# Query-chunk and value-row stores moved between the GpSimd and SP queues, and the second attention head loaded later, in a hybrid attention layer

## The chip, the cores and the metric

The kernel runs on one core of a Trainium2 chip. The metric is the device time of one execution in microseconds; a kernel's time is the median of its runs. The engines are named as the profile names them: PE is TensorE (matrix products into PSUM banks), PEld its weight loads, DVE is VectorE, ACT is ScalarE, POOL is GpSimd, SP is SyncE, which only issues transfers. A transfer is issued by an instruction on one of these engines. Those that SP issues are in the profile's DMA queue q1, those that GpSimd issues in q0; sixteen DMA engines carry both.

## The reference

One layer of a decoder trunk on 1024 tokens of width 1024 with 16 meta tokens ahead of them, all in float32. One input projection feeds two groups of heads: four gated-DeltaNet heads and eight forgetting-attention heads of width 64. One output projection takes both, then comes a SwiGLU network of inner width 2816 and a last norm:

```
u = rmsnorm(h, attn_norm_w[l])
proj = u @ w_in[l]
gq, gk, gv, gz, gb, ga, fq, fk, fv, ff = jnp.split(proj, IN_SPLITS, axis=-1)
o_gdn = gated_deltanet_group(...)
o_fox = forgetting_attention_group(fq, fk, fv, ff, fgate_b[l])
h = h + jnp.concatenate([o_gdn, o_fox], axis=-1) @ w_out[l]
h = h + swiglu(rmsnorm(h, ffn_norm_w[l]), w_gate[l], w_up[l], w_down[l])
h = rmsnorm(h, final_norm_w)
return h[:, N_META:]
```

and in the attention group, by blocks of 128 queries (the meta tokens are a block of their own),

```
sc = einsum("bqhd,bkhd->bhqk", q[:, s:e], k[:, :e]) * scale + c[:, :, s:e, None] - c[:, :, None, :e]
p = softmax(where(causal, sc, MASK_VALUE), axis=-1)
outs.append(einsum("bhqk,bkhd->bqhd", p, v[:, :e]))
```

where `c` is the running sum of the logarithms of the forget gates.

## The kernel before

Each float32 product is made of three products of rounded parts: a value is split into a high part (`hi`, a cast on ACT) and a low part (`lo`, a subtraction on DVE), and PE adds hi·hi, hi·lo and lo·hi into one PSUM bank.

The program runs in stages: the DeltaNet projections (0 to 230 us of the span); the attention heads' value projection in two blocks of four heads, `fv1` (230 to 259.5) and `fv0` (259.5 to 285); their key projection `fk` (to 345), with the DeltaNet group's triangular solves (`py`, `pu`) between its matmuls; their query projection `fq` (to 433.5), with the DeltaNet group's eight scan chunks between; the attention (to some 580), in which output-projection matmuls of the DeltaNet half (`wog`) fill the gaps; the rest of the output projection (to 658); and the SwiGLU network.

The order of PE's instructions is set by a small planner (`PeOrder`, L45): chains of work with due times are taken when due, and a filler (`fox()`, the attention heads' projections, later `wog`) is taken otherwise. PE takes that order as it stands. On the other engines and the queues the order is the scheduler's, which takes instructions by priority as their inputs come. `tc.issue_after(x)` puts what is issued in its scope behind the instruction `x` on the engine on which `x` is queued; it is an order on that queue and does not wait for the transfer to land.

What the change touches:

- `fox_proj` (L762) projects keys, then queries. For each pair of heads `m` (0 to 3) and each of three column chunks it fills a PSUM bank (`pj_fq`), splits it into the tile `fhl_fq{m}_{c0}` (ACT L777, DVE L778; two buffers) and stores that to a DRAM scratch, `k_d` or `q_d` (L780, on GpSimd). The three PSUM banks that `ps_mm` hands out in turn are shared with `wog`. The names in the rows are `fhl_fq2_358` for pair 2, column 358, and so on; `fq3_700` is the last.
- The value blocks (L937 to L959) come as nine row tiles each: the 16 meta rows (tile -1) and eight of 128 tokens. Each is split into a tile `fvt` (three buffers) and stored to DRAM: the meta rows by four small stores to `vz_d` (L953), the others to `v_d` (L957), on SP. `vst[0]` holds the last such store; the loads of the key projection's weights (`raw_fk0`, `raw_fk1`), and `ubk` and `na` of the solves (L605 to L608), are issued behind it.
- `att_tiles(i)` (L725) makes the score operands `ka{i}` and `qa{i}` and fills six rows of each with constants on GpSimd (L727, L728). `att_head(h)` (L739) loads a head on SP: the gate sums into `ka` and `qa`, two halves each of `kk` and `sa`, the rest of `ka` and `qa`, the values `avt`, and then the meta values `vm0`/`vm1` (`vm_load`, L736; head 1 brings those of heads 0 and 1). The buffers alternate between even and odd heads. The scores read `ka`, `qa`, `kk`, `sa`; the products with the meta rows' probabilities (`phm`) read `vm`, the others `avt`.
- `wout_gdn` (L1179) loads a tile of the input `x` as `ht` (L1190, GpSimd), runs twelve `wog` matmuls, adds the one to the other on DVE (L1193) and stores the sum to `h_d` (L1194, GpSimd).
- `zmask` (L1013, L1014) is the causal mask of the scores, filled on GpSimd; the casts `whi_wo` and `wlo_wo` (L168, L169) split output-projection weights into the buffers in which the query projection's weights were.

Of the kernel before, what the change touches and what calls it, by code (L numbers as in the profile page):

```python
# [9 lines left out]
F32 = mybir.dt.float32  # L10
# [11 lines left out]
NT = S // P  # L22
# [75 lines left out]
def tile_hymba_layer(ctx, tc, x, meta, attn_norm_w, w_in, conv_w, a_log, dt_bias, gdn_norm_w,  # L98
                     fgate_b, w_out, ffn_norm_w, w_gate, w_up, w_down, final_norm_w, out):
    nc = tc.nc  # L100
    x, out, w_in, conv_w = x[0], out[0], w_in[0], conv_w[0]
# [12 lines left out]
    def ps_mm(name):  # L114
        rot[0] = rot[0] % 3 + 1 if rot[0] else 0
        return ps_v(name) if rot[0] > 1 else bank("mm", 1, name)
# [34 lines left out]
    v_d = dram.tile([FH, T, P], F32, name="v_d")  # L151
# [58 lines left out]
    def mm3g(dst, pairs, us):  # L210
        n = len(pairs)
        for i, (lh, ll, rh, rl) in enumerate(pairs):
            for a, b, first, last in ((lh, rh, i == 0, False), (lh, rl, False, False), (ll, rh, False, i == n - 1)):
                nc.tensor.matmul(dst, a, b, start=first, stop=last)  # L214
                od.pe(us)
                yield
# [56 lines left out]
    def tok_cols(t):  # L273
        return (0, NM) if t < 0 else (NM + P * t, P)
# [431 lines left out]
    def proj_tmg(acc, t, w, n):  # L706
        col, rows = tok_cols(t)
        yield from mm3g(acc[:rows, :n], [(uh[:, k, col:col + rows], ul[:, k, col:col + rows], w[0][k][:, :n],
                                          w[1][k][:, :n]) for k in range(KT)], n / 2400)

    last, vst = [None], [None]
# [5 lines left out]
    def fox_load():  # L717
        if fox_ws:
            with tc.issue_after(vst[0].ins) if vst[0] and not last[0] else nullcontext():
                fox_w.append(win_block(*fox_ws.pop(0)))  # L720

    t_ld, hds, fixed, fq_m, h_ld = [], {}, [], [0], {}

    def att_tiles(i):
        ka = als[i].tile([NA + DH, T], F32R, name=f"ka{i}")  # L725
        qa = als[i].tile([NA + DH, S], F32R, name=f"qa{i}")
        nc.gpsimd.memset(ka[:NA].bitcast(F32), 1.0)  # L727
        nc.gpsimd.memset(qa[:NA].bitcast(F32), -1.0)  # L728
        fixed.append((ka, qa))
# [4 lines left out]
    def vm_load(h):  # L734
        for i in range(2):
            h_ld[h] = nc.sync.dma_start(vms[h % 2][NR * i:NR * i + NR].rearrange("p j c -> p (j c)").bitcast(F32),  # L736
                                        vz_d[h, 0:NR * 512].rearrange("(p f) -> p f", f=512))

    def att_head(h):  # L739
        m, hb = h // 2, h % 2  # L740
        rows = slice(DH * hb, DH * hb + DH)
        al_ = als[h % 2]
        kk = al_.tile([P, T], F32R, tag="kk", name=f"kk_{h}")
        sa = al_.tile([P, S], F32R, tag="sa", name=f"sa_{h}")
        ka, qa = fixed[h % 2]
        nc.sync.dma_start(ka[3:NA].bitcast(F32), c_d[h])
        nc.sync.dma_start(qa[0:3].bitcast(F32), c_d[h, :, NM:T])
        for i in range(2):
            half = slice(DH * i, DH * i + DH)
            nc.sync.dma_start(kk[half].bitcast(F32), k_d[m, rows, 0])  # L750
            nc.sync.dma_start(sa[half].bitcast(F32), q_d[m, i, rows])
        nc.sync.dma_start(ka[NA:].bitcast(F32), k_d[m, rows, 1])
        nc.sync.dma_start(qa[NA:].bitcast(F32), q_d[m, 0, rows])
        vt = al_.tile([P, NT, P], F32R, tag="vt", name=f"avt_{h}")
        nc.sync.dma_start(vt.bitcast(F32), v_d[h, NM:T].rearrange("(t p) d -> p t d", p=P))
        t_ld.append(od.t)
        if h:
            for i in (0, 1) if h == 1 else (h,):
                vm_load(i)
        return m, rows, kk, sa, ka, qa, vt  # L760

    def fox_proj(dst, chunks, off, scale, nm):  # L762
        for b in range(2):
            w = fox_w.pop(0)
            for i in range(2):
                m = 2 * b + i
                for ci, (c0, n) in enumerate(chunks):
                    if (i, ci) == (0, 1):
                        fox_load()
                    acc = ps_mm(f"pj_{nm}{m}_{c0}")  # L770
                    yield from mm3g(acc[:, :n], [(w[0][k][:, P * i:P * i + P], w[1][k][:, P * i:P * i + P],
                                                  uh[:, k, c0:c0 + n], ul[:, k, c0:c0 + n])
                                                 for k in range(KT)], n / 2400)
                    od.on("act", n / 1200)
                    od.on("dve", n / 900)
                    hl = fp.tile([P, 2, 348], F32R, tag="fhl", name=f"fhl_{nm}{m}_{c0}")
                    nc.scalar.activation(hl[:, 0, :n], acc[:, :n], AF.Copy, scale=scale)  # L777
                    nc.vector.scalar_tensor_tensor(hl[:, 1, :n], acc[:, :n], scale, hl[:, 0, :n].bitcast(F32),  # L778
                                                   op0=ALU.mult, op1=ALU.subtract)
                    last[0] = nc.gpsimd.dma_start(dst(m)[:, :, c0 - off:c0 - off + n], hl[:, :, :n].bitcast(F32))  # L780
                    if off:
                        fq_m[0] = m

# [28 lines left out]
    ra_ld = {}  # L812
# [116 lines left out]
    def fox():  # L929
        fox_load()  # L930
        w = fox_w.pop(0)
        for t in range(NT):
            if t == 1:
                fox_load()
            acc = ps_mm(f"z0_{t}")
            yield from proj_tmg(acc, t, w, 256)
            gate_out(t, acc, *((fvp, "fvt") if t < NT - 2 else (fp, "fhl")), 0)  # L937
        for b in (1, 0):
            n = 256 + 8 * b
            w = fox_w.pop(0)  # L940
            for t in range(-1, NT):
                if t == (3 if b else 1):
                    fox_load()
                col, rows = tok_cols(t)
                acc = (ps_mm if b or t % 2 else ps_t)(f"fv{b}_{t}")
                yield from proj_tmg(acc, t, w, n)
                vt = fvp.tile([P, 4, 2, DH], F32R, tag="fvt", name=f"fvt{b}_{t}")
                av = acc[:rows, :256].rearrange("p (h d) -> p h d", d=DH)
                split(vt[:rows, :, 0], vt[:rows, :, 1], av)
                src = vt[:rows].rearrange("p h a d -> p h (a d)").bitcast(F32)  # L950
                if t < 0:
                    for j in range(GRP):
                        vst[0] = nc.sync.dma_start(  # L953
                            vz_d[4 * b:4 * b + 4, VZ * j:VZ * j + NM * 512].rearrange(
                                "h (r f) -> r h f", f=512)[:, :, 0:P], src)
                else:
                    vst[0] = nc.sync.dma_start(v_d[4 * b:4 * b + 4, col:col + rows].rearrange("h t d -> t h d"), src)  # L957
                if b:
                    nc.vector.tensor_copy(fr[:rows, NT if t < 0 else t], acc[:rows, 256:264])  # L959
        fvc.close()  # L960
        yield from fox_proj(lambda m: k_d[m], TCH, 0, 1.0, "fk")
        od.add(csum(), od.t + 8.0)
        yield from fox_proj(lambda m: q_d[m].rearrange("a p c -> p a c"), ((NM, 342), (NM + 342, 342), (NM + 684, 340)), NM, -DH ** -0.5, "fq")

    lv_left, outs_left = {0, 1}, set(range(NT))
# [21 lines left out]
    als.append(alc.enter_context(tc.tile_pool(name="alo", bufs=1)))  # L987
    for i in range(2):
        vms.append(als[1].tile([P, GRP, P], F32R, name=f"vm{i}"))
    att_tiles(1)  # L990
    hds[1] = att_head(1)
    while od.step_fill():
        pass
    uctx.close()

    atc = ExitStack()
# [180 lines left out]
    h_st = []  # L1177

    def wout_gdn(nb, tt):  # L1179
        if nb not in wvs:  # L1180
            parts_n[0] = 2 if nb else 1
            with tc.issue_after(ra_ld[2].ins) if not nb else nullcontext():
                wvs[nb] = wout_block(0, nb, col=gnw)
            parts_n[0] = 1
            od.on("act", 2.2)
            od.on("dve", 3.2)
        cols, nbc = slice(P * tt, P * tt + P), slice(512 * nb, 512 * nb + 512)
        ht = wo.tile([P, 512], F32, tag="ht", bufs=5, name=f"ht_{tt}_{nb}")
        with tc.issue_after(h_st[-2].ins) if len(h_st) >= 2 else nullcontext():
            nc.gpsimd.dma_start(ht, x[cols, nbc])  # L1190
        acc = ps_mm(f"wog_{tt}_{nb}")
        yield from mm3g(acc, gdn_pairs(tt, nb), 0.2135)
        V.tensor_add(ht, acc, ht)  # L1193
        h_st.append(nc.gpsimd.dma_start(h_d[tt, :, nbc], ht))  # L1194
        yield od.on("dve", 0.6)
# [3 lines left out]
    def wout_gdn_all(part):  # L1199
        for nb, tt in part:  # L1200
            yield from wout_gdn(nb, tt)
# [545 lines left out]
```

## Time and profile before

| what | us |
|---|---|
| median of 3 runs | 1297.9 (1297.64 to 1297.99) |
| the profiled execution | 1296.32 |
| its span, first to last instruction | 1294.6 |
| PE busy | 1277.3 |
| PE busy in `fv0`, 259.5 to 285 | 25.50 of 25.50 |
| PE busy in `fk`, 285 to 345 | 60.00 of 60.00 |
| PE busy in `fq`, 345 to 433.5 | 88.50 of 88.50 |
| PE busy in the attention, 433.5 to 580 | 141.54 of 146.50 |
| mean granted clock of PE | 0.998 |

All numbers of one row of the trace come from the one profiled execution. A row of a timeline begins with its start and its length in us; behind the operation, in brackets, stands the idle time before it and what ended it. Matmuls overlap, so the distance between two starts, not the length, is what one costs.

### The profile page before, as it was taken

How to read it: one execution, taken by the hardware profiler on the slowest of the kernel's cores; microseconds unless marked ns; L12 is line 12 of the kernel's file. 1: busy time of each engine (PE TensorE's matmuls, PEld its weight loads, DVE VectorE, ACT ScalarE, POOL GpSimd, SP SyncE). 2: the span in 40 equal slices, each digit the busy share in tenths (PEclk: the TensorE clock that was granted, in tenths of full speed). 3: DMA queues.
4: the chain of work that ended last, by engine and by line, in shares of the span. 5: the costliest groups of instructions: out<-in, count | busy, mean ns of one | idle time of the engine just before them, and what ended most of it. 6: DMA issues, size and time to landing. Idle time of an engine off the chain costs nothing.

```text
span 1294.6 us, 19961 instructions
## 1 busy us (share of the span) xinstructions
PE 1277.3 (99%) x7434; PEld 1126.3 (87%) x7434; DVE 840.4 (65%) x1508; ACT 546.3 (42%) x940; POOL 367.9 (28%) x342
## 2 busy tenths in 40 slices
PE   8999999999999999999999999999999999999998
PEld 8999999999999888887778888888888888888887
DVE  6567899574267488886887666655656664465645
ACT  6455444133234477884453323333333343433332
POOL 2012213102333212213405534455433453020301
PEclk9999999999999999999999999999999999999999
DMA  6433634677498778838434654553445468945513
GB/s 231 133 114 116 178 93 105 171 199 225 151 338 260 200 217 222 226 79 269 163 130 153 196 165 147 179 187 130 147 155 170 156 212 290 375 179 201 208 63 130
DMA packets 181840, 234.90 MB, mean 181 GB/s; under 512 B 19160, under 2 KB 132080, under 8 KB 178928
## 3 DMA queue, kind: packets, MB, share of 16 engines
q1 hardware_dynamic: 176048, 215.74, 52.0%
q0 software_dynamic: 5696, 17.90, 4.2%
q8 instruction: 58, 0.95, 0.3%
q14 instruction: 38, 0.31, 0.1%
HBM read 154.68 MB, written 78.92 MB: 180 GB/s over the span
## 4 chain that ended last, share of the span: by engine, by line
PE 89%; DMA 4%; DVE 3%; issue 2%; ACT 1%; POOL 1%; SPq 1%; POOLq 0%; DVEq 0%; ACTq 0%
PE xp L1628 9%; PE yp L1628 7%; PE ua L1453 5%; PE ga L1453 5%; PE gb L1453 5%; PE ud L1453 5%; PE gd L1453 5%; PE ub L1453 5%; PE pj_fk L214 4%; PE fv L214 3%; PE pt L1071 2%; PE ue L1453 2%; PE ge L1453 2%; PE wog L214 2%; PE z L214 2%
## 5 line engine op out<-in xcount | busy, mean ns | idle before, releaser
L166 DVE TENSOR_TENSOR al_p<-ra_p,ah_p 128x2048 fp32r<-128x2048 f32 (+1 forms) x21 | 46.6, 2221 | 93.9 <-ACT ah_p L165 93.9
L165 ACT CAST ah_p<-ra_p 128x2048 fp32r<-128x2048 f32 (+1 forms) x21 | 37.1, 1766 | 106.0 <-PE xp L1628 48.5
L1628 PE MATMUL xp<-wh_p,al_p 128*128 128x512 f32 (+1 forms) x176 | 67.3, 382 | 0.0
L1628 PE MATMUL xp<-wl_p,ah_p 128*128 128x512 f32 (+1 forms) x176 | 67.3, 382 | 0.0
L1628 PE MATMUL xp<-wh_p,ah_p 128*128 128x512 f32 (+1 forms) x176 | 67.3, 382 | 0.0
L1509 POOL TENSOR_TENSOR gzw<-gzw,uzt 128x512 f32<-128x512 f32 x11 | 18.4, 1676 | 164.9 <-DVE uzt L1498 113.6
L1453 PE MATMUL gb<-uh_p,w_g_p 128*128 128x512 f32 x176 | 57.8, 389 | 0.0
L1453 PE MATMUL ub<-uh_p,w_u_p 128*128 128x512 f32 x176 | 57.8, 389 | 0.0
L1453 PE MATMUL gd<-uh_p,w_g_p 128*128 128x512 f32 x176 | 57.8, 389 | 0.0
L1453 PE MATMUL ud<-uh_p,w_u_p 128*128 128x512 f32 x176 | 57.8, 389 | 0.0
L1509 POOL TENSOR_TENSOR gxy<-gxy,uxy 128x512 f32<-128x512 f32 x22 | 38.3, 1740 | 66.5 <-DVE uxy L1498 58.7
L166 DVE TENSOR_TENSOR w_u_p<-raw_u,w_u_p 128x512 fp32r<-128x512 f32 x42 | 43.2, 1027 | 20.3 <-ACT w_u_p L165 20.1
L165 ACT CAST ph<-pt 128x512 fp32r<-128x512 f32 (+1 forms) x96 | 45.4, 477 | 23.4 <-PE pt L1071 20.6
L166 DVE TENSOR_TENSOR pl<-pt,ph 128x512 fp32r<-128x512 f32 (+1 forms) x96 | 51.9, 553 | 4.5 <-ACT ph L165 4.0
L1035 ACT ACTIVATE pr<-pr,sm 128x144 f32<-128x144 f32 (+3 forms) x64 | 50.6, 793 | 6.0 <-DVE sm L1030 5.7
L1453 PE MATMUL ua<-uh_p,w_u_p 128*128 128x512 f32 x160 | 52.5, 389 | 0.0
L1453 PE MATMUL ga<-uh_p,w_g_p 128*128 128x512 f32 x160 | 52.5, 389 | 0.0
L1628 PE MATMUL yp<-wh_p,ah_p 128*128 128x512 f32 x132 | 51.3, 389 | 0.0
L1628 PE MATMUL yp<-wl_p,ah_p 128*128 128x512 f32 x132 | 51.3, 389 | 0.0
L1628 PE MATMUL yp<-wh_p,al_p 128*128 128x512 f32 x132 | 51.3, 389 | 0.0
L165 ACT CAST w_u_p<-raw_u 128x512 fp32r<-128x512 f32 x42 | 26.0, 620 | 55.3 <-PE gd L1453 35.6
L166 DVE TENSOR_TENSOR wl_p<-rw_p,wh_p 128x2048 fp32r<-128x2048 f32 (+1 forms) x21 | 46.9, 2235 | 3.4 <-ACT wh_p L165 3.4
(651 smaller groups left out, 4250.0 us busy)
## 6 DMA issues: line engine op xcount, KB each, us to landing
ra_p<-ao_p SPq DMA_DIRECT2D x14, 1024.0 KB
raw_g<-in_w_gate_dram SPq DMA_DIRECT2D x22, 512.0 KB
raw_u<-in_w_up_dram SPq DMA_DIRECT2D x22, 512.0 KB
raw_d<-in_w_down_dram SPq DMA_DIRECT2D x22, 512.0 KB
wt_p<-raw_d SPq DMA_DIRECT2D x33, 256.0 KB
rw_p<-wt_p SPq DMA_DIRECT2D x8, 1024.0 KB
rw_p<-in_w_down_dram SPq DMA_DIRECT2D x6, 1024.0 KB
ao_p<-gzw SPq DMA_DIRECT2D x22, 256.0 KB
```

The source lines that it names most:

```text
L165: cast = nc.scalar.copy(dst_hi, src)
L166: low = nc.vector.tensor_sub(dst_lo, src, dst_hi.bitcast(F32))
L214: nc.tensor.matmul(dst, a, b, start=first, stop=last)
L1035: nc.scalar.activation(pr[:, :n], pr[:, :n], AF.Exp, bias=sm[:, np_ - 1:np_], scale=-1.0, accum_out=rsum[:, h, j:j + 1])
L1071: nc.tensor.transpose(pt[:, P * j:P * j + P], pts[j][0][:, j, c0:c0 + P], ident)
L1453: nc.tensor.matmul(dst, a[:, c], b[:, k], start=(first and k == 0 and i == 0), stop=(k == 3 and i == 2), skip_group_check=not first)
L1509: last_mul[0] = G.tensor_tensor(gs[d], gs[d], us[d], op=ALU.mult)
L1628: nc.tensor.matmul(dst[:, n_], a[:, f, c], b[:, f, n_], start=(first and i == 0 and n == 0), stop=(i == NF - 1 and n == 2), skip_group_che ...
```

## The change

Four edits. The store of a key or query chunk goes through GpSimd while scan chunks are still to be done (`outs_left` is not empty) and through SP after that. The rows of `fv0` are stored through GpSimd, those of `fv1` through SP as before, and `vst[0]` is the last store of `fv1`. The tiles `ka1`/`qa1` and the loads of head 1 are put behind the last query store (`last[0]` as it stands at the one place and the other), and the loads are issued after the remaining steps of the query projection. The first two `ht` loads go through SP, behind the load `ra` of the last scan chunk.

```diff
-                    last[0] = nc.gpsimd.dma_start(dst(m)[:, :, c0 - off:c0 - off + n], hl[:, :, :n].bitcast(F32))
+                    last[0] = (nc.gpsimd if outs_left else nc.sync).dma_start(dst(m)[:, :, c0 - off:c0 - off + n], hl[:, :, :n].bitcast(F32))
...
-                        vst[0] = nc.sync.dma_start(
+                        st_ = (nc.sync if b else nc.gpsimd).dma_start(
...
-                    vst[0] = nc.sync.dma_start(v_d[4 * b:4 * b + 4, col:col + rows].rearrange("h t d -> t h d"), src)
+                    st_ = (nc.sync if b else nc.gpsimd).dma_start(
+                        v_d[4 * b:4 * b + 4, col:col + rows].rearrange("h t d -> t h d"), src)
+                if b:
+                    vst[0] = st_
...
-    att_tiles(1)
-    hds[1] = att_head(1)
+    with tc.issue_after(last[0].ins):
+        att_tiles(1)
     while od.step_fill():
         pass
+    with tc.issue_after(last[0].ins):
+        hds[1] = att_head(1)
...
-        with tc.issue_after(h_st[-2].ins) if len(h_st) >= 2 else nullcontext():
-            nc.gpsimd.dma_start(ht, x[cols, nbc])
+        early = len(h_st) < 2
+        with tc.issue_after((ra_ld[NT - 1] if early else h_st[-2]).ins):
+            (nc.sync if early else nc.gpsimd).dma_start(ht, x[cols, nbc])
```

PE's order of instructions is the same in both kernels. SP's queue at the end of the query projection and the start of the attention, before (`avt_0` ends the first head's loads; `kk_1` begins the second's):

```order
L755 DMA avt_0_4715<-v_d_106 128x8x128
L750 DMA kk_1_4873<-k_d_105 64x1040
L751 DMA sa_1_4874<-q_d_104 64x1024
L746 DMA ka1_4869<-c_d_108 3x1040
L750 DMA kk_1_4873<-k_d_105 64x1040
L747 DMA qa1_4870<-c_d_108 3x1024
L751 DMA sa_1_4874<-q_d_104 64x1024
L752 DMA ka1_4869<-k_d_105 64x1040
L753 DMA qa1_4870<-q_d_104 64x1024
L755 DMA avt_1_4883<-v_d_106 128x8x128
L736 DMA vm0_4867<-vz_d_107 64x512 x2
L736 DMA vm1_4868<-vz_d_107 64x512 x2
```

and now:

```order
L755 DMA avt_0_4715<-v_d_106 128x8x128
L1196 DMA ht_0_0_5005<-in_x_dram 128x512
L1196 DMA ht_1_0_5041<-in_x_dram 128x512
L780 DMA q_d_104<-fhl_fq2_700_4873 128x2x340
L780 DMA q_d_104<-fhl_fq3_16_4902 128x2x342
L780 DMA q_d_104<-fhl_fq3_358_4931 128x2x342
L780 DMA q_d_104<-fhl_fq3_700_4960 128x2x340
L746 DMA ka1_4869<-c_d_108 3x1040
L747 DMA qa1_4870<-c_d_108 3x1024
L750 DMA kk_1_4964<-k_d_105 64x1040
L751 DMA sa_1_4965<-q_d_104 64x1024
...
L755 DMA avt_1_4974<-v_d_106 128x8x128
L736 DMA vm0_4867<-vz_d_107 64x512 x2
```

Six transfers that GpSimd issued now stand between the first head's loads and the second's, and the second head's `vm0` comes after its `avt_1` as before. GpSimd's queue at the same place, before (`os_7` is work of the last scan chunk):

```order
L220 TENSOR_TENSOR os_7_4794<-os_7_4794,mhalf_94 128x4
L727 MEMSET ka1_4869 6x1040
L728 MEMSET qa1_4870 6x1024
L1190 DMA ht_0_0_5005<-in_x_dram 128x512
L1190 DMA ht_1_0_5041<-in_x_dram 128x512
L780 DMA q_d_104<-fhl_fq2_358_4826 128x2x342
L780 DMA q_d_104<-fhl_fq2_700_4889 128x2x340
L780 DMA q_d_104<-fhl_fq3_16_4918 128x2x342
L1013 MEMSET zmask_5023 128x1040
L780 DMA q_d_104<-fhl_fq3_358_4947 128x2x342
L1014 AFFINE_SELECT zmask_5023<-zmask_5023 128x128
L780 DMA q_d_104<-fhl_fq3_700_4976 128x2x340
```

and now:

```order
L220 TENSOR_TENSOR os_7_4794<-os_7_4794,mhalf_94 128x4
L780 DMA q_d_104<-fhl_fq2_358_4826 128x2x342
L727 MEMSET ka1_4869 6x1040
L728 MEMSET qa1_4870 6x1024
L1018 MEMSET zmask_5023 128x1040
L1019 AFFINE_SELECT zmask_5023<-zmask_5023 128x128
L1200 DMA h_d_4989<-ht_0_0_5005 128x512
```

One query store is left there, now ahead of the memsets. GpSimd's queue in the value block `fv0` now (before, none of these stores was on it):

```order
L953 DMA vz_d_107<-fvt0_-1_3030 16x4x128 x4
L957 DMA v_d_106<-fvt0_0_3062 128x4x128
L957 DMA v_d_106<-fvt0_1_3103 128x4x128
L585 MEMSET amt_2423 4x256
L586 MEMSET amt_2423 4x16
L957 DMA v_d_106<-fvt0_2_3146 128x4x128
L957 DMA v_d_106<-fvt0_3_3175 128x4x128
L586 MEMSET amt_2423 4x16
L957 DMA v_d_106<-fvt0_4_3204 128x4x128
```

The stores of tiles 5 to 7 and then the first key stores follow. On SP the loads `raw_fk0`, `ubk_0`, `na_0`, `na_1` and `raw_fk1` stand directly behind the last store of `fv1`, where before they stood between the stores of `fv0`; on ACT the casts of `raw_fk0` stand ahead of the casts of the value tiles 0 and 1.

## The prediction

> **What bounds the kernel now.** I read the page's busy shares first, then the waits of TensorE, then its timeline and the granted clock around the longest wait, then the chain of waits that leads there. The page says that TensorE works nearly all of the span:
>
> ```profile
> span 1294.6 us, 19961 instructions
> PE 1277.3 (99%) x7434; PEld 1126.3 (87%) x7434; DVE 840.4 (65%) x1508; ACT 546.3 (42%) x940; POOL 367.9 (28%) x342
> ```
>
> So only TensorE's idle time and lowered clock can be won, and anything else counts once TensorE waits for it. The longest wait of TensorE, from its list of waits (total, times, longest):
>
> ```profile
> PE wog L214 <- DVE fhl_fq L778: 1.9, 1, 1.9
> ```
>
> It lies where the query projection (`pj_fq`) ends and the attention stage begins with output-projection matmuls (`wog`) and the first scores (`sc`), as TensorE's timeline shows:
>
> ```profile
> 433.27 0.31 PE L214 MATMUL pj_fq<-uh,wlo_fq 128*128 128x340 f32 x1
> 435.48 0.58 PE L214 MATMUL wog<-whi_wo,uh_p 128*128 128x512 f32 x1 [1.89 <-DVE fhl_fq L778]
> 435.85 0.63 PE L214 MATMUL wog<-wlo_wo,uh_p 128*128 128x512 f32 x1
> 436.28 0.63 PE L214 MATMUL wog<-whi_wo,ul_p 128*128 128x512 f32 x1
> 439.69 0.39 PE L214 MATMUL wog<-whi_wo,ul_p 128*128 128x512 f32 x1
> 439.93 0.23 PE L1025 MATMUL sc<-ka,qa 70*128 70x144 f32 x1
> ```
>
> Behind the wait the first of twelve `wog` matmuls follow each other at 0.43 us, the last at 0.24. The windows (TensorE busy and count, then weight loads, DVE, ACT, POOL, granted clock, DMA share, GB/s) name the reason, a clock of one half:
>
> ```profile
> 436.00:439.00 3.00, 3.00 (x9) 2.32 (x8) 2.73 (x5) 1.66 (x4) 2.59 (x4) 0.50 0.51 174
> 439.00:440.00 1.00, 1.00 (x7) 0.81 (x5) 0.22 (x1) 0.45 (x1) 0.00 (x0) 0.92 0.88 338
> 440.00:442.00 2.00, 1.87 (x12) 1.36 (x11) 1.64 (x7) 0.85 (x4) 1.30 (x3) 1.00 0.04 10
> ```
>
> What the stall hangs on stands in the chain of waits:
>
> ```profile
> 425.32 8.99 DMA q_d<-fhl_fq
> 434.42 0.47 ACT fhl_fq L777
> 434.91 0.53 DVE fhl_fq L778
> ```
>
> A query store, issued on GpSimd at 425.32, takes 8.99 us to land. Until then its buffer (`fhl`, two buffers) is not free, the PSUM bank of `fq3_16` cannot be emptied, and the first `wog` needs that bank. Ahead of it on GpSimd were two memsets, which waited for SP's loads, and two `ht` loads. What GpSimd and SP did in the meantime (timelines; start, duration):
>
> ```profile
> 419.62 0.96 POOL L727 MEMSET ka<- 6x1040 f32 x1 [1.58 <-DMA qa<-q_d]
> 424.09 1.16 POOL L1190 DMA_DIRECT2D ht<-in_x_dram  x2 [2.63 <-issue]
> 419.65 0.46 SPq L750 DMA_DIRECT2D kk<-k_d  x1
> 426.98 4.32 SPq L736 DMA_DIRECT2D vm<-vz_d  x4
> ```
>
> The second head's loads were issued from 419.65 (`kk`) to 431.3 (`vm`) and filled the DMA engines just while the store tried to leave.
>
> **Term 1: the stall at 433.5 goes.** In the change `fq2_358` is stored on GpSimd ahead of the memsets, the three stores behind it and the last one go through SP, and the second head's loads are behind them all. The DVE row
>
> ```profile
> 419.42 0.51 DVE L778 SCALAR_TENSOR_TENSOR fhl_fq<-pj_fq,fhl_fq 128x342 fp32r<-128x342 f32 x1
> 422.98 0.45 ACT L777 ACTIVATE fhl_fq<-pj_fq 128x340 fp32r<-128x340 f32 x1 [4.30 <-DMA q_d<-fhl_fq]
> ```
>
> puts the first at 419.95 and the next at about 424. Even if it takes 8.99 us again, it has landed at 428.9, and `fq3_16` is out of its bank by 430, 3.5 us before TensorE needs it. I therefore take the whole stall as gone. From start to start: the next matmul could follow 433.27 after 0.16 us, twelve `wog` at 0.23 to 0.24 us end at 436.2, and `sc` starts there and not at 439.93: **-3.7 us** (1.9 idle, 1.8 of half clock). If the store were held up all the same, the whole stall would stay; the 3.5 us of room speak against it.
>
> **Edits that I cost at nothing.** The two `ht` loads take 0.6 us of issue each on SP at 419.7, where nothing else is queued until 424, and are read only behind the first `wog` group, at 434. The memsets of `ka1` and `qa1` (0.96 us each) run from about 420.7, and what follows them on SP comes after 436. `zmask` (a memset of the same length and a select of one tile, 1.5 us as an estimate) waits for the last `pj_fq` and is there at 435.1, before the first score at 436.2. Earlier key weights in the first value phase find TensorE without a gap (25.50 of 25.50 us busy in the window below): no gain. Without that cover each would cost its own duration, 1 to 2 us.
>
> **Term 2: the second head's loads are late.** They now stand behind the store of `fq3_700`. Its projection ends at 433.6 on TensorE; ACT and DVE keep four casts of `wo` weights ahead of it, and the last two wait for the buffers of that same projection's weights. Their rows of before (pairs):
>
> ```profile
> 436.33 1.32 ACT L168 ACTIVATE whi_wo<-raw_wo,gnw 128x512 fp32r<-128x512 f32 x2
> 437.27 1.46 DVE L169 SCALAR_TENSOR_TENSOR wlo_wo<-raw_wo,gnw,whi_wo 128x512 fp32r<-128x512 f32 x2
> ```
>
> 433.6, ACT's pair of 1.3, half of DVE's pair behind it, 0.75, and the tile's own subtraction, 0.5: the store leaves at 436.2 and the first load at 436.65, 17 us later than 419.65. The same burst for a later head is there to be timed:
>
> ```profile
> 485.00 0.26 SPq L746 DMA_DIRECT2D ka<-c_d  x1
> 489.42 0.96 SPq L753 DMA_DIRECT2D qa<-q_d  x1
> 494.00:497.00 3.00, 3.00 (x20) 2.65 (x18) 2.57 (x6) 1.23 (x4) 0.79 (x2) 1.00 1.04 231
> 497.00:499.00 2.00, 2.00 (x15) 1.84 (x14) 1.84 (x6) 1.89 (x4) 1.12 (x2) 1.00 0.74 240
> vm<-vz_d SPq DMA_DIRECT2D x4, 128.0 KB
> ```
>
> From the first issue at 485.00 the engines are full until about 497.3: 12.3 us for nine loads, `avt` among them. On 436.65 this gives 448.9 for `avt_1`; `vm0`, two of the last row's loads, is behind it: 0.26 MB at the 231 GB/s of the window, 1.1 us, 450.0. The store of `fq3_700` in the same queue delays them by up to 0.6 us (an estimate: 0.35 MB at that rate is 1.5 us, and the loads' issue hides 0.9): 450.0 to 450.6. I take 450.4, since the store is surely there. When are they needed? TensorE's order does not change, so its rows of before tell it:
>
> ```profile
> 451.26 0.32 PE L1025 MATMUL sc<-ka,qa 70*128 70x144 f32 x1
> 451.80 0.56 PE L1092 MATMUL po<-phm,vm 128*128 128x128 f32 x4
> ```
>
> Less the 3.7 us won, the second head's first score comes at 447.5 and `po` with `vm0` at 448.1. The score's data is on the bus ahead of `avt_1`, until about 446.5: in time by 1 us. `vm0` is not: TensorE, in order, stands 450.4 - 448.1 = **+2.3 us** at `po`, with the first head's remaining work and everything of the second head queued behind it. Bounds: no wait if `vm0` lands by 448.1, which needs a burst of 10.0 us instead of 12.3 (windows of 174 to 338 GB/s stand above, so that this is not excluded); 4.9 us if GpSimd's `h_d` stores and `ht` loads, which fall into the same stretch, take another fifth of the engines from it, 2.6 us.
>
> **Term 3: does the clock fall again?** The 1.89 us of idle time above ended in 3 us at 0.50. The next shorter wait is harmless:
>
> ```profile
> 608.51 0.47 PE L204 MATMUL wof<-whi_wo,ohl 128*128 128x512 f32 x1 [0.84 <-DVE hst L1278]
> 609.00:610.00 1.00, 1.00 (x6) 0.78 (x6) 0.90 (x2) 0.87 (x1) 0.00 (x0) 1.00 0.86 307
> ```
>
> 0.84 us costs no clock, 1.89 us does; 2.3 us is beyond the upper row, so I add what the first stall cost, **+1.8 us**.
>
> **Sum**: -3.7 + 2.3 + 1.8 = +0.4 us on the span of 1294.6. The profiled execution itself took 1296.32 us and the median of the runs is 1297.9, 1.6 above it; with the same distance the change comes to 1296.7 and 1298.3 us. About 0.2%, 2.6 us, is what a measurement of this kernel can tell from no change; I forecast no change that can be measured.
>
> [...]
>
> **The rivals.**
>
> *The gain is kept* (chance 0.25). If the second head's burst takes 10 us or the last store leaves by 434.5, `vm0` is there by 448.1 to 449, the wait at `po` stays under the 0.84 us that cost no clock, and 2.9 to 3.7 us are won: 1294.2 to 1295.0, say 1294.5. For it: from 440 to 442 the DMA engines were at 0.04 in before, so the burst has them to itself at first. Against it: the burst of the later head took 12.3 us beside like GpSimd traffic.
>
> *Slower: value stores starve on GpSimd* (chance 0.1). The stores of the first value projection leave by GpSimd while SP's key weights, `na` and `ubk` fill the DMA engines. A window of just this kind of competition shows what comes of it:
>
> ```profile
> q1 hardware_dynamic: 1876, 1.29, 105.6%
> k_d<-fhl_fk POOLq DMA_DIRECT2D x1, 348.0 KB, 7.3
> k_d<-fhl_fk POOLq DMA_DIRECT2D x1, 346.0 KB, 6.5
> ```
>
> In 294 to 298 all that moved was SP's queue, and GpSimd's stores took 6.5 and 7.3 us. The value tiles have three buffers (`fvt`), so the cast of tile 7 waits for the store of tile 4, and that for the store of tile 1. In before tile 1 was cast at 269.69; two key-weight casts now stand ahead of it, and I put its store 3 us behind that, at 272.7. With 1.3 us per cast, subtraction and issue, tile 7 is cast at 275.3 plus two landings. Behind it on ACT are a key-weight cast, a key tile and the copies that TensorE's `pu` matmuls read:
>
> ```profile
> 269.69 0.35 ACT L165 CAST fvt<-fv 128x256 fp32r<-128x256 f32 x1
> 290.40 0.37 ACT L165 CAST fvt<-fv 128x256 fp32r<-128x256 f32 x1 [0.58 <-DMA v_d<-fvt]
> 291.96 1.16 ACT L633 COPY y<-py 32x512 f32<-32x512 f32 x2
> 293.02 0.66 PE L640 MATMUL pu<-y,tb 32*32 32x32 f32 x22
> 259.50:285.00 25.50, 25.50 (x219) 1.00 0.65 172
> ```
>
> There is no room after 290.40. It decides from a landing of 7.5 us on: at 7.0 us tile 7 is cast at 289.3, at 9.0 us at 293.3, a stall of 2.9 us with 1.8 us of half clock, on top of the sum: 1303.0. Against it: 6.5 and 7.3 are both under 7.5.
>
> [...]
>
> *No second halving of the clock* (chance 0.1): the second stall costs 2.3 us alone, -3.7 + 2.3 = -1.4, 1296.5. Against it is the 1.89 us row.
>
> *Slower: the burst is held up* (chance 0.1): `vm0` lands 2.6 us later still, the upper bound of term 2, -3.7 + 4.9 + 1.8 = +3.0, 1300.9.
>
> **How the numbers follow.** The forecast has 0.45: 1298.3, its own range 1296.9 to 1299.7 (1.4 us on either side for the landing of `vm0`). Faster by over 0.2%: 0.25, the first rival. Slower: 0.2, the starved stores and the held-up burst. Within: 0.55, the forecast and the rival on the clock. The range reaches from the first rival's 1294.2 to the held-up burst's 1301.2 and leaves out the starved stores and the tails.
>
> **What would show it.** In the changed kernel TensorE's list should have no wait of `wog` on `fhl_fq`, and the first `sc` should start 3.7 us earlier after the last `pj_fq`. SP's first load of the second head should be at 436 to 437, and `po` at L1097 (L1092 before) should wait some 2.3 us for the DMA of `vm`, with PEclk at 0.50 behind it. If that wait is under 1 us, terms 2 and 3 are wrong and the kernel is faster. If `fvt` on ACT waits for `v_d` until after 290, and `pu` at L640 waits, the second rival is the case.

## The result: slower by 0.8%, and the profile after

| | us |
|---|---|
| before, median of 4 runs | 1297.95 (1297.64 to 1298.7) |
| the change, median of 4 runs | 1308.87 (1307.31 to 1311.66) |
| ratio | 1.0084, 95% interval 1.0069 to 1.0099 |
| span of the change's profiled execution | 1305.7 (before 1294.6) |
| mean granted clock of TensorE | 0.992 (before 0.998) |

The forecast was 1298.3 us, with a range to 1301.2. The change takes 10.9 us more than the kernel before. TensorE's list of waits in the changed kernel (total, times, longest):

```profile
PE po L1097 <- DMA vm<-vz_d: 3.7, 1, 3.7
PE sc L1030 <- DMA qa<-c_d: 2.3, 1, 2.3
...
PE pu L640 <- ACT y L633: 1.2, 2, 0.8
...
PE pj_fk L214 <- DVE fvt L166: 1.0, 1, 1.0
```

The wait of `wog` on `fhl_fq` is gone. In its place there are four others at two places, and both places had been named: the second head's operands, and the value block's stores.

**At the value block**, GpSimd's timeline in the changed kernel (start, length, idle time before it and what ended it):

```profile
271.75 0.78 POOL L957 DMA_DIRECT2D v_d<-fvt  x1 [2.98 <-DVE spl_f L342]
278.73 0.76 POOL L957 DMA_DIRECT2D v_d<-fvt  x1 [6.19 <-issue]
...
284.43 0.75 POOL L957 DMA_DIRECT2D v_d<-fvt  x1 [4.47 <-issue]
287.45 0.76 POOL L957 DMA_DIRECT2D v_d<-fvt  x1 [2.27 <-issue]
```

and DVE's and ACT's:

```profile
273.34 0.42 DVE L166 TENSOR_TENSOR fvt<-fv,fvt 128x256 fp32r<-128x256 f32 x1
```

```profile
278.44 0.37 ACT L165 CAST fvt<-fv 128x256 fp32r<-128x256 f32 x1 [3.60 <-DMA v_d<-fvt]
284.22 0.37 ACT L165 CAST fvt<-fv 128x256 fp32r<-128x256 f32 x1 [5.41 <-DMA v_d<-fvt]
...
293.31 0.37 ACT L165 CAST fvt<-fv 128x256 fp32r<-128x256 f32 x1 [1.71 <-DMA v_d<-fvt]
```

Tile 1 was ready at 273.76, but its store was issued at 278.73, after 6.19 us for which the trace shows no cause on GpSimd. What happened just before is on ACT's row: at 278.44 the cast of tile 3 started because the store of tile 0 had landed. So did the next two: the casts that wait for a landing start at 284.22 and 287.25, and GpSimd issues at 284.43 and 287.45. GpSimd issued each store only when the one before it was through: the seven stores behind the first were issued 0.30 to 0.39 us after the landing of the one before, and 3.5 to 8.2 us after their own tile was ready. The last tile was cast at 293.31 in place of 290.40. PE then had gaps, and the clock fell behind them:

```profile
290.05 0.42 PE L214 MATMUL pj_fk<-uh,whi_fk 128*128 128x346 f32 x1 [0.99 <-DVE fvt L166]
295.49 0.24 PE L640 MATMUL pu<-y,tb 32*32 32x32 f32 x2 [0.84 <-ACT y L633]
296.09 1.19 PE L640 MATMUL pu<-y,tb 32*32 32x32 f32 x62 [0.36 <-ACT y L633]
```

```profile
298.00:300.00 2.00, 2.00 (x8) 2.00 (x8) 1.86 (x6) 0.46 (x1) 0.00 (x0) 0.50 0.80 280
```

**At the start of the attention**, PE's and SP's timelines:

```profile
438.00 0.31 PE L214 MATMUL pj_fq<-uh,wlo_fq 128*128 128x340 f32 x1
438.15 0.39 PE L214 MATMUL wog<-whi_wo,uh_p 128*128 128x512 f32 x1
440.90 0.23 PE L1030 MATMUL sc<-ka,qa 70*128 70x144 f32 x1
...
454.70 0.30 PE L1030 MATMUL sc<-ka,qa 70*128 70x144 f32 x1 [2.28 <-DMA qa<-c_d]
459.61 1.09 PE L1097 MATMUL po<-phm,vm 128*128 128x128 f32 x4 [3.70 <-DMA vm<-vz_d]
```

```profile
427.69 13.52 SPq L780 DMA_DIRECT2D q_d<-fhl_fq  x4
441.31 0.29 SPq L746 DMA_DIRECT2D ka<-c_d  x1
...
446.50 5.35 SPq L736 DMA_DIRECT2D vm<-vz_d  x4
```

The last `pj_fq` is followed by `wog` after 0.15 us, and the twelve take 2.75 us, 0.23 each. The second head's first load is issued at 441.31, its last score data is there at 454.7, `vm` at 459.5, and TensorE stands twice. The granted clock (third number from the end, behind the engines' busy times) falls between the two waits and stays down until 465:

```profile
452.00:454.00 2.00, 0.41 (x3) 0.14 (x1) 0.59 (x3) 1.51 (x3) 0.00 (x0) 1.00 1.08 213
456.00:459.00 3.00, 0.00 (x0) 0.00 (x0) 0.14 (x1) 0.41 (x3) 0.00 (x0) 0.50 1.04 225
460.00:464.00 4.00, 4.00 (x18) 3.79 (x18) 1.23 (x5) 0.88 (x3) 0.00 (x0) 0.50 1.03 235
```

### The profile page after: what moved, and what is told of

Its sections match the earlier page's. It is cut to its first block, busy times and chain, and to the rows that moved or that the text cites. A ratio compares the mean times of both kernels' runs of the same rounds, so it can differ in the third digit from the quotient of the medians.

```text
span 1305.7 us, 19965 instructions
## 1 busy us (share of the span) xinstructions
PE 1281.9 (98%) x7434; PEld 1129.6 (87%) x7434; DVE 840.3 (64%) x1508; ACT 547.2 (42%) x940; POOL 371.7 (28%) x348
## 4 chain that ended last, share of the span: by engine, by line
PE 86%; DMA 4%; DVE 4%; issue 3%; ACT 1%; SPq 1%; POOL 0%; POOLq 0%; DVEq 0%; ACTq 0%
PE xp L1634 9%; PE yp L1634 7%; PE ua L1459 5%; PE ga L1459 5%; PE gb L1459 5%; PE ud L1459 5%; PE gd L1459 5%; PE ub L1459 5%; PE pj_fq L214 3%; PE pj_fk L214 3%; PE ue L1459 2%; PE ge L1459 2%; PE pt L1076 2%; PE z L214 2%; PE wog L214 1%
```

## The experiments

All are compared with the kernel before, run on the same chip beside them; its median was 1297.3 to 1297.8 us in the three groups. TensorE's order of instructions is the same in all of them.

| kernel | median us | ratio to before, 95% interval |
|---|---|---|
| the change, again | 1309.09 | 1.0086 (1.0069 to 1.0103) |
| value rows back on SP | 1301.6 | 1.0023 (1.0014 to 1.0033) |
| value rows alone moved | 1305.7 | 1.0051 (1.0037 to 1.0064) |
| second head earlier | 1300.93 | 1.0021 (1.0010 to 1.0032) |
| value rows whole | 1302.65 | 1.0031 (1.0021 to 1.0041) |
| half of the value rows on GpSimd | 1306.47 (one run) | |
| `vm` first in the burst | 1301.44 | 1.0032 (1.0020 to 1.0044) |
| both parts undone | 1295.99 | 0.9990 (0.9980 to 0.9999) |
| whole rows and head earlier | 1295.95 | 0.9990 (0.9981 to 1.0000) |
| both undone, burst cut | 1293.32 | 0.9963 (0.9950 to 0.9977) |
| whole rows, burst cut | 1293.91 | 0.9973 (0.9963 to 0.9984) |

The theory after the result: three separate pieces, a gain of 3.7 us (the query stores), a loss at the value block, a loss at the second head. Its rivals: one of the two losses does nothing by itself; the value block's loss comes from the loads that were moved ahead, not from the queue; the late burst is slow wherever it stands.

### The change once more

> The changed kernel itself, once more, beside the others of this group. Both theories: 1308 to 1309 us as at first; the waits of po on vm and of sc on qa between 2 and 4 us.

It took 1309.09 us, with waits of 2.65 us on `qa` and 3.70 us on `vm`.

### Value rows back on SP

```diff
-                        st_ = (nc.sync if b else nc.gpsimd).dma_start(
+                        st_ = nc.sync.dma_start(
...
-                if b:
-                    vst[0] = st_
+                vst[0] = st_
```

> The change with one part undone: the rows of the first value block are stored through SP again, and the loads stand behind its last store again. Theory (two separate losses, the value stores on GpSimd +4.6 us in the stretch 285 to 302, the late second head +10.2 us at its first score and at the products with vm, against a gain of 3.7 us at the end of the query projection): 1308.9 - 4.6 = 1304.3 us, with no wait of pu and pj_fk in the trace and the waits of sc on qa and of po on vm unchanged at 2.3 and 3.7 us. Rival (the value stores cost nothing by themselves, the second head's lateness is everything): 1308.9 us.

1301.6 us: 7.3 to 7.5 us less than the change, more than the 4.6 expected, and far from the rival. PE's rows of this kernel:

```profile
436.15 0.23 PE L1029 MATMUL sc<-ka,qa 70*128 70x144 f32 x1
449.86 0.30 PE L1029 MATMUL sc<-ka,qa 70*128 70x144 f32 x1 [2.20 <-DMA qa<-q_d]
454.53 1.09 PE L1096 MATMUL po<-phm,vm 128*128 128x128 f32 x4 [3.81 <-DMA vm<-vz_d]
```

The first score starts 3.78 us earlier than before (436.15 against 439.93), which is the gain of the moved query stores and `ht` loads undisturbed. Of the 2.7 us by which the time falls further than expected, the clock has some 1.5 by estimate: at the second head it is at one half for 6.8 us here, 3.6 of them busy, and for 10.2 us in the change, 6.5 of them busy. The two waits are as long as in the change, so that they are a loss of their own.

### Value rows alone moved

The kernel before with the value rows' two stores through GpSimd for the block `fv0` (the "first" of the expectation, since it holds heads 0 to 3) and `vst[0]` set by `fv1` alone, as in the diff of the change.

> The kernel before with this one part added: the first value block's rows are stored through GpSimd and the loads stand behind the last store of the other block. Theory: 1297.9 + 4.6 = 1302.5 us, GpSimd's stores each issued only when the one before has landed, waits of pj_fk and pu on PE of about 1.0 and 1.2 us and half a clock behind them. Rival: 1297.9 us, no wait there.

1305.7 us (1301.1 to 1308.4), 3 us above the expectation. The waits of `pj_fk` (0.95) and `pu` (0.85 and 0.36) are there, with two of `py` on DVE (1.6 us together) that the second trace of the change has too, and the stall at the end of the query projection became another one: `wog` does not wait, but the second score does, because DVE's queue has the last `fhl_fq` ahead of the first softmax:

```profile
447.45 0.70 PE L1028 MATMUL sc<-ka,qa 70*128 70x400 f32 x1 [3.96 <-DVE sm L1033]
```

So this part alone makes the kernel slower; the exact size depends on what it shifts behind it.

### Second head earlier

```diff
     while od.step_fill():
-        pass
-    with tc.issue_after(last[0].ins):
-        hds[1] = att_head(1)
+        if 1 not in hds and stl[-1] == "fq3_16":
+            with tc.issue_after(last[0].ins):
+                hds[1] = att_head(1)
```

(`stl` holds the names of the stores issued so far.)

> The change with the second head's loads put behind the third query store from the end (pair 3, first chunk) in place of the last one; the last two query stores stand behind them on SP. Theory: the loads start near 432 in place of 441, their last score data lands by 446 and vm by 451, before PE asks for them (452.4 and 452.8), so both waits and the half clock behind them go: 1308.9 - 10.2 = 1298.7 us. Rival (the burst is slow because the DMA engines are shared with GpSimd's transfers and the next head's loads, wherever it stands): a wait of po on vm stays, over 1302 us.

1300.93 us; 8 us less than the change. Both waits are gone: the second head's first score and `po` with `vm` start with no idle time ahead of them (456.90 and 457.45). Two things kept it 2 us above the expectation. In its profiled execution the half clock behind the value block lasted longer (a granted clock of 0.86 over 285 to 310, against 0.93 in the change), and a new wait of 1.26 us stood in front of the meta rows' transpose, on ACT's copy of `pm`. The next kernels show where that comes from.

### Value rows whole

```diff
-    v_d = dram.tile([FH, T, P], F32, name="v_d")
+    v_d = dram.tile([FH // GRP, T, GRP * P], F32, name="v_d")
...
-                        v_d[4 * b:4 * b + 4, col:col + rows].rearrange("h t d -> t h d"), src)
+                        v_d[b, col:col + rows], src.rearrange("p h d -> p (h d)"))
```

The load of `avt` reads its head's columns of the new layout, in pieces of 512 bytes as before.

> The change with another layout of the scratch tensor for the values: the four heads of a block lie side by side, so that a store of one row tile is 128 pieces of 2 KB in place of 512 pieces of 512 bytes; bytes, queue and order are the same. Theory A (GpSimd's queue holds only so many pieces, and the next store waits for room): stores are issued as soon as their tile is subtracted, tile 7 is cast before 289, no wait of pj_fk and pu: 1308.9 - 4.6 = 1304.3 us. Rival B (a store on GpSimd waits for the landing of the one before whatever its pieces, or the DMA engines are full with SP's loads): as the change, 1308.9 us.

1302.65 us, 6.2 to 6.4 us less than the change, by the layout of the rows alone. GpSimd's timeline:

```profile
271.87 0.58 POOL L957 DMA_DIRECT2D v_d<-fvt  x1 [2.98 <-DVE spl_f L342]
274.16 0.75 POOL L957 DMA_DIRECT2D v_d<-fvt  x1 [1.71 <-DVE fvt L166]
...
277.29 0.54 POOL L957 DMA_DIRECT2D v_d<-fvt  x1 [0.75 <-DVE fvt L166]
279.14 0.54 POOL L957 DMA_DIRECT2D v_d<-fvt  x1 [1.32 <-DVE fvt L166]
```

Every store is now issued 0.29 to 0.45 us after its own tile is ready; tile 7 is cast at 286.49, and no wait of `pj_fk` or `pu` is left. The stores do not land faster. From issue to landing they took 4.5 us in the median here and 3.0 in the change, each over its eight stores:

```profile
DMA to landing us min/median/max: 2.3/4.5/6.1
```

```profile
DMA to landing us min/median/max: 2.7/3.0/6.6
```

So it was the issue that waited, and neither the loads that had been moved ahead (they are the same here) nor the transfer.

### Half of the value rows on GpSimd

In the change each store of a row tile is cut in two; heads 0 and 1 go through GpSimd (256 pieces of 512 bytes), heads 2 and 3 through SP:

```diff
+                    for j in range(0, 4, 4 if b else 2):
+                        e = nc.gpsimd if not (b or j) else nc.sync
```

> The change with each value store of the first block cut in two: heads 0 and 1 through GpSimd (256 pieces of 512 bytes), heads 2 and 3 through SP. Theory A (GpSimd's queue takes up to some number of pieces in flight between 768 and 1023, and an issue waits for room): at most 256 + 256 + 256 pieces are in flight, so GpSimd issues each store when its tile is subtracted, with no idle of 2 to 6 us that nothing in the trace explains. Theory B (it is the small piece that is slow on GpSimd): the unexplained idle times between the stores stay at half their size or more. The time itself may be anything from 1301 to 1309 us, since SP's halves stand behind its loads.

```profile
271.44 0.74 POOL L960 DMA_DIRECT2D v_d<-fvt  x1 [2.90 <-DVE spl_f L342]
273.74 0.77 POOL L960 DMA_DIRECT2D v_d<-fvt  x1 [1.56 <-DVE fvt L166]
...
277.02 0.72 POOL L960 DMA_DIRECT2D v_d<-fvt  x1 [0.90 <-DVE fvt L166]
282.27 0.71 POOL L960 DMA_DIRECT2D v_d<-fvt  x1 [4.53 <-DVE fvt L166]
```

With pieces of the old size and half their number each store is issued 0.29 to 0.49 us after its tile is ready; where GpSimd is idle, DVE's tile was late (the 4.53 us, since the buffer's other half was still in SP's queue behind the loads). The whole rows moved the same bytes without the waits, and here the pieces are as small as in the change: what the waits go with in these runs is the number of pieces in flight. The rest fits: 256 + 512 and 512 + 256 were taken in the change without a wait (the four `vz_d` stores and tile 0; tile 7 and the first key store), and 512 + 512 never, nor the 256 after those last 768. Counted from issue to landing, the most that GpSimd has in flight is 896 pieces, in the kernel before (at 493.54 and 532.60) as in the change (at 543.06), and never 1024. What it does between the two was not tried.

### `vm` first in the burst

On the kernel with the value rows back on SP, the loads of `vm0` and `vm1` stand ahead of the second head's other loads.

> As the kernel with the value rows back on SP (1301.6 us, waits of 2.2 us on qa and 3.8 us on vm, then 3.4 us lost to the clock), but in the late burst the loads of vm0 and vm1 stand ahead of the second head's other loads. Theory A (transfers of a queue land about in the order of issue): the wait on vm goes, the wait on qa grows by the 0.5 MB now ahead of it at 230 GB/s, 2.2 us, to 4.4 us; one stall over 2 us, so the clock still falls: 1301.6 - 1.6 = 1300.0 us. Theory B (the loads in flight share the engines, so that all end at the end of the burst): a wait of some 6 us on qa in one piece, 1301.6 us.

```profile
PE sc L1031 <- issue: 6.0, 1, 6.0
```

1301.44 us, and one wait of 6.0 us in place of 2.2 and 3.8 (the trace names no releaser for it). The second head's first score starts at 453.57; with the old order all was there for `po` at 454.53. That is Theory B's number, but not its mechanism. The chain of waits of this kernel (start, length) has a `vm` load that is through at 443.11, ten microseconds ahead of the first score:

```profile
437.58 5.53 DMA vm<-vz_d
443.13 8.39 DMA ka<-k_d
```

By the landings in the two traces: with `vm` first, its four loads land at 439.48 to 445.32, the last score load at 453.38 and `avt` at 456.67; with the old order, the last score load lands at 449.51, `avt` at 453.38 and `vm` at 453.86 to 455.06. So Theory A had the order of the landings and missed the size: its 2.2 us are the bytes of `vm`, and the last score load moved by 3.9. GpSimd's four transfers (1.05 MB) are in flight beside SP's: with `vm` first all four land ahead of the last score load, with the old order two. The sum of the waits stays since the second head's score and `po` together need nearly the whole burst in either order: what the new order puts behind the deadline is `avt`, and what it puts ahead is `vm1`, a difference of 0.26 MB or, as an estimate with the 230 GB/s of 441 to 460 in the change, 1.1 us (453.38 against 454.40, where `vm0` landed).

### Both parts undone

> The change with the value rows back on SP and the second head's loads behind pair 3's first query store: what is left are the query stores' move to SP and the two x loads. Theory (the query stores' move is worth the 3.7 us that the first score came earlier, and both losses are gone): 1297.4 - 3.7 = 1293.7 us, no wait over 1 us between 430 and 460. Rival (something else in the new order costs too): 1296 to 1298 us.

1295.99 us, 0.9990 of before: faster, but by a third of what was expected. ACT's rows of this kernel name what took the rest:

```profile
448.28 0.24 ACT L1045 COPY pm<-pr 128x64 f32<-128x64 f32 x1 [5.47 <-DMA q_d<-fhl_fq]
```

The last two query stores now stand on SP behind the second head's burst, and the last of them lands behind it: `pm`'s copy waits 5.47 us for that, until 448.28, and TensorE 1.58 us for `pm`.

### Whole rows and head earlier

The change with both repairs, the layout and the earlier head.

> The whole change with both repairs: the value rows stay on GpSimd but as 128 pieces of 2 KB, and the second head's loads stand behind pair 3's first query store. Theory (pieces and lateness are all that the change lost): 1293.7 us, as with both parts undone. Rival (GpSimd's stores cost something in other ways): 1295 us or more, with a wait of PE between 285 and 302.

1295.95 us, like the one above: nothing of the value block's loss is left when the rows are whole. The wait on `pm` is there too (1.33 us).

### Both undone, burst cut

The values' loads of a head (`avt`, `vm`) become a function of their own; for the second head it is called behind the last query store:

```diff
                 hds[1] = att_head(1)
+    with tc.issue_after(last[0].ins):
+        load_values(1, hds[1][6])
     uctx.close()
```

> As the kernel with both parts undone (1296.0 us, in which the copy of pm on ACT waits 5.2 us for the last query store, which stands on SP behind the second head's burst), but the burst is cut: the eight loads for the scores behind pair 3's first query store, then the last two query stores, then avt_1 and the vm loads. Theory (the rest of the gain was lost in that wait): the last store lands by 441, pm does not wait, pt of the meta rows does not wait, avt_1 and vm are there by 447: 1296.0 - 2.3 = 1293.7 us. Rival (the gain at the first score is swallowed later by the softmax on DVE in any case): 1296.0 us, first score some 3.5 us earlier and no wait, but the second head's first score as late as before.

1293.32 us, 0.9963 of before (0.9950 to 0.9977), faster than both kernels. SP's and PE's rows:

```profile
427.96 0.30 SPq L752 DMA_DIRECT2D ka<-c_d  x1
...
432.49 4.34 SPq L784 DMA_DIRECT2D q_d<-fhl_fq  x2
436.88 0.46 SPq L740 DMA_DIRECT2D avt<-v_d  x1
```

```profile
436.49 0.23 PE L1036 MATMUL sc<-ka,qa 70*128 70x144 f32 x1
...
447.79 0.32 PE L1036 MATMUL sc<-ka,qa 70*128 70x144 f32 x1
448.32 0.56 PE L1103 MATMUL po<-phm,vm 128*128 128x128 f32 x4
```

The gain of 3.44 us at the first score (436.49 against 439.93) is still 3.48 at `po` with `vm` (448.32 against 451.80). `pm` waits 1.55 us for the last store here, and that holds nobody up. The rival, that the softmax swallows the gain, is out.

### Whole rows, burst cut

> The same with the value rows on GpSimd in pieces of 2 KB. Theory: the same time as the kernel beside it, 1293.7 us, as the value block does not set the end either way. Rival: GpSimd's issue or the earlier key loads gain or lose over 1 us.

1293.91 us; its interval overlaps with the one above. With whole rows no difference between the two queues can be measured.

## Why the prediction was wrong, point by point

The same instructions' starts, against before, give the ledger of the changed kernel's profiled execution. The first score started at 439.93 before, at 440.90 in the change, and at 436.15 with the value rows back on SP.

| step | predicted us | measured us | how |
|---|---|---|---|
| term 1, the stall goes | -3.7 | -3.8 | 436.15 - 439.93 |
| value rows on GpSimd | 0 (second rival: +4.7) | +4.8 | 440.90 - 436.15 |
| term 2, second head late | +2.3 | +6.0 | 2.28 + 3.70 |
| term 3, half clock behind it | +1.8 | +3.5 | head 1's `po` with `vm`, 471.35 - 460.93, less 0.97 and 5.98 |
| all that is behind it | 0 | +0.7 | remainder to 1305.7 - 1294.6 |
| sum | +0.4 | +11.1 | |

**Term 1 was right** in mechanism and size; in the change itself the first score comes 2.90 us after the last `pj_fq`, and 6.66 before. TensorE waits for none of the edits that I costed at nothing, though they were not undone one by one. The sum held nothing for the value rows, which I had put among the rivals.

**The choice between forecast and second rival failed first.** I gave the starved stores a chance of 0.1 and tied them to one number, a landing time over 7.5 us. The place and the chain (three buffers, tile 7 on tile 4 on tile 1, ACT's copies, `pu`) were right. The condition was not, and that the price came out (4.7 against 4.8, tile 7 cast at 293.3 against 293.31) is luck: I had two landings of 9.0 us, and the trace has landings of 5.4 and 2.7 with stores issued 5.0 and 5.4 us late between them. The stores landed in 2.7 to 6.6 us, well under 7.5, and the loss came all the same, because a store was not issued until the one before had landed. I had counted 0.7 us for the issue. Nothing in the trace of before showed a store of 512 pieces on GpSimd; its key and query stores have 256 each. I took their issue times for a store with twice the pieces, and no bound was set on the issue itself. A sign of this was there to be read, in the attention of the kernel before:

```profile
494.75 0.62 POOL L1103 DMA_DIRECT2D o_d<-oa  x1 [0.59 <-issue]
```

With three such stores of 256 pieces in flight, the fourth was issued 0.3 us after the first of them landed (494.43).

**Term 2 was mis-sized.** Its start was right: the first load was issued at 441.31 where I had 436.65, and the value block's delay of 4.75 us accounts for that. The end was not. The score data took 13.3 us from the first issue (454.6 - 441.31) where I had 9.9, and `vm` 18.2 us where I had 13.8. The score data was to be in time by 1 us and became a wait of 2.28, and the wait on `vm` was 3.70 in place of 2.3. I had read 12.3 us for nine loads off the windows of a later head; the last of those nine landed only 13.9 us after the first issue (498.93 against 485.00). To that I added 0.6 us for a store that is 1.5 us of bytes by my own figures, and nothing for the `vm1` loads, which land together with `vm0` (459.07 to 460.24). The transfers from 441 to 460 of the change:

```profile
q1 hardware_dynamic: 2220, 3.33, 73.9%
q0 software_dynamic: 320, 1.05, 16.6%
```

These are 4.38 MB in 19 us, 230 GB/s, the rate on which I had reckoned. The store (0.35 MB), the nine loads (2.13 MB), the four `vm` loads (0.52 MB) and GpSimd's four transfers (1.05 MB) are 4.05 MB; at that rate they take 17.6 us, close to the measured 18.2. From a first load at 436.65 this estimate has `vm` there at 454.2, a wait of 6.1 us in place of 2.3. The share of GpSimd's transfers can be seen by itself: with both parts undone the burst is ahead of them, and from its first issue to the last `vm` load it takes 14.6 us (429.64 to 444.23), where it takes 18.9 in the change (441.31 to 460.24). The upper bound of 4.9 us, which was the fourth rival, did not hold the measured 6.0; its mechanism, GpSimd's `h_d` and `ht` transfers beside the burst, is part of what happened.

**Term 3 had the right sign.** The clock fell, and the rival without a second halving is out. I had taken over the cost of one stretch of half clock, 3.4 us long in the kernel before; in the change the stretch lasted 10.2 us (455 to 465), with two waits 4.9 us apart, and cost 3.5 in place of 1.8.

**The first rival** (burst of 10 us, gain kept) is out. Its condition was reached otherwise, by starting the burst 9 us earlier (427.96 against 436.56 with the value rows back on SP) and cutting it: 1293.3 us, where it had 1294.5.

## What to carry to other kernels

A transfer that is moved to another queue brings its number of pieces along: before a store goes to GpSimd, count its pieces, and lay the data out so that a row is one piece (here 1302.65 us in place of 1308.87). For a deadline in a burst, add up the bytes that stand ahead in the same queue and, beside them, what the other queue moves until then (here 4.05 MB, 17.6 us at the measured 230 GB/s, for a burst that took 18.2); putting one load first did not help here, since what it overtook was wanted at the same time (1301.44 us and 1301.6). And when a stall is removed, a load that was early enough beside the stall has to be moved forward, or cut so that what is wanted first is not tied to what is wanted last (here 1293.32 us, with both parts undone and the burst cut).

## What the runs showed of the hardware that was not expected

In the kernel before and in the change GpSimd had at most 896 pieces in flight and never 1024. At the change's value block it stands for 1.6 to 6.2 us until a store has landed; for four of these eight waits the trace names no cause, for the others a DVE instruction, though the tile had been ready for 3.5 us or more. With whole rows another issuer made no difference that can be measured: 1295.95 us on GpSimd and 1295.99 us on SP. With 512 pieces it did: the change takes 6.2 to 6.4 us more than with whole rows.

In the burst from 441 to 461 of the change, SP's transfers of 128 KB and more landed in the order of their issue: the last score load at 454.50, `avt` at 458.29, `vm` at 459.07 to 460.24. Two loads of 12 KB issued at 452.47 and 453.44 landed at 459.73 and 460.08, ahead of the last `vm` load, which was issued at 451.41. So it was in the burst with `vm` first, in which the first `vm` load was through 14 us before the last score load (439.48 and 453.38).

In the traces of the kernel before and of the change the granted clock is 1.00 or 0.50. The stretches at 0.50, but for the one at each kernel's end, lasted 3.41 us (from 435.76 before, from 11.20 and 297.92 in the change) and 10.24 us (from 454.93 in the change). The length of one wait alone does not explain them. In the 3.41 us before the fall TensorE was busy for 1.52 us in the kernel before, and for 1.13 at the second head of the change. At the change's value block it was busy for 2.21 of 3.41 us, with idle times of only 0.84 and 0.36 us, among `pu` matmuls of 32x32, and the clock fell all the same. A wait of 1.58 us among full-sized matmuls (both parts undone) left the clock at 1.00 from 430 to 470. In the same kernel TensorE was busy for all of the 85.00 us from 345 to 430, and the mean granted clock there was 0.98. How much the idle time, its place and the size of the products count was not tried. The first wait of 2.28 us at the second head's score was enough: the clock was at 0.50 from 454.93 on, before the second wait began at 455.91.

How long the clock stayed down differed between two executions of nearly the same work: over 285 to 310 its mean was 0.93 in the change and 0.86 with the second head earlier, which is some 1.7 and 3.5 us. The waits ahead of it were not quite the same: the first was 0.99 and 0.61 us, and with the second head earlier one of 1.19 us, for `py`, came on top.
